# Right-side SBUF tiles moved down by 32 bytes in a hybrid encoder block on one core

## The chip, the core and the metric

The kernel runs on one core of one Trainium2 chip. The metric is the device time of one execution in microseconds, and the time of a kernel is the median of its runs. A profiled execution also gives a span, from the first to the last instruction on the core, which is a little shorter than the device time.

## What is computed

One layer of a bidirectional encoder is applied to two batches with shared weights: a prompt of 512 tokens and a sample of 256, which the kernel treats as 768 rows. The width is 2048 and everything is float32.

```
h = rmsnorm(x); z = h @ w_in                  # [fourier 1024 | q 1024 | k 256 | v 256]
of = fourier_mix(zf, w_f)                     # Re(2-D DFT over positions, channels), 8 groups
q, k = rope(q), rope(k)                       # 16 query heads, 4 key heads, width 64
oa = window_attention(q, k, v, sink)          # each token sees +-128 positions, plus a sink
x = x + concat(rmsnorm(of), rmsnorm(oa)) @ w_out
h = rmsnorm(x)
u = relu(h @ w_up); x = x + (u * u) @ w_down  # 2048 -> 8192 -> 2048
y = rmsnorm(x)
```

## The kernel before

Every large product is done as three matmuls on TensorE. Each operand is split into a high part (rounded to the format that the matmul reads, by ScalarE) and a low part (the rest, by VectorE), and high x high, high x low and low x high are added in PSUM. In the profile, tiles with an `h` at the end of the name hold high parts, those with an `l` low parts.

The work goes through these stages, in this order.

- **v** (line 222): the value projection, accumulated for all six blocks of 128 rows. The result is split into `vhl`.
- **z** (line 546): the input projection. A weight piece `wh` or `wl` is the stationary operand (the one that is loaded into the array, the profile's PEld rows), and a half of the rows, 384 columns of `hh` or `hl`, is the moving operand (the one that streams through). The Fourier group (lines 331, 363, 384) and the rotation of keys and queries are interleaved.
- **attention and first output projection**: scores (line 588, stationary `qs`, moving `kdl` or `kdh`), transposes of the probabilities (line 642), their product with the values (line 659, stationary `vhl`, moving `th` or `tl`), between steps of the output projection (line 743, 512 moving columns of `wh` or `wl`). A planner written in the kernel sets the order of this stage. The second half of the output projection follows, with transposes of its result (line 132), which fill `xf`.
- **up** (line 1038): `h @ w_up` with a seven-product scheme of the Strassen kind. Stationary are `wh` and `wl`, moving are 384 columns of `xf`, or of `xs` for one of the seven products in the second half.
- **down** (line 1325): `(u*u) @ w_down`, 512 moving columns of `wh` or `wl`, then the final norm and the stores.

SBUF holds 128 partitions, and a tile occupies the same bytes of each. Tile pools are stacked from two ends: most of them from the low addresses up (left), and those opened with `side="right"` from the high addresses down. These are the pools on the right:

```python
vp = vctx.enter_context(tc.tile_pool(name="vp", bufs=1, side="right", reuse_waits="tile"))
vhl = vp.tile([P, NM, NKV, 2, HD], F32R, tag="vhl", name="vhl")
...
kp = kt["kp"] = kctx.enter_context(tc.tile_pool(name="kp", bufs=1, side="right", reuse_waits="tile"))
...
tp = tctx.enter_context(tc.tile_pool(name="tp", bufs=1, side="right", reuse_waits="tile"))
xf = tp.tile([P, 7, 2, 4, HALF], F32R, tag="xf", name="xf")
...
bp = bctx.enter_context(tc.tile_pool(name="bp", bufs=1, side="right", reuse_waits="tile"))
```

`kp` holds the mask, the tables of the rotation (`cosr`, `sinr`), `sink`, the keys (`kdh`, `kdl`), the rotation's work tiles (`rx`, `ry`, `rh`, `rl`) and the queries (`qs`). `bp` holds `cx`, from which `xf` is split. A fifth pool on the right holds `xs`, which takes the first of the seven factors of the second half while `xf` is still in use. `vp` and `kp` are closed after the attention, and `tp` then starts at the same edge.

The right edge lies at byte 229344 of a partition, which is 32 more than a multiple of 64. Every tile on the right has a size that is a multiple of 64 bytes, so each of them starts at 32 more than a multiple of 64: `vhl` at 217056, `kdl` at 187360, `kdh` at 175072, `xf` at 143328, `xs` at 131040. On the left most tiles that matmuls read start at a multiple of 64 (`wh` from 9984, `wl` from 30464, `hh` from 59136, `hl` from 71424, `th`, `tabh`, `cwh`); those of the Fourier group behind an odd-sized tile (`sh` at 195360, `sl`, `ah`, `al`, `ofh`, `ofl`) start at 32 more.

The matmul of the up stage and the reads of its moving operand:

```python
xb = right[kh][s]          # xf[:, factor], in the second half also xs
for t in range(2):
    for i in range(4):
        for n, (w, o) in enumerate(((wh, 0), (wh, 1), (wl, 0))):
            nc.tensor.matmul(ps[:, t, :HALF], w[:, i, t * P : (t + 1) * P], xb[:, o, i, :], ...)
```

Of the kernel before, what the change touches and what calls it, by code (L numbers as in the profile page):

```python
# [11 lines left out]
F32 = mybir.dt.float32  # L12
# [8 lines left out]
P = 128  # L21
# [19 lines left out]
def hybrid_encoder(ctx: ExitStack, tc: tile.TileContext, a: dict):  # L41
# [7 lines left out]

    cpool = ctx.enter_context(tc.tile_pool(name="cpool", bufs=1))  # L50
    wpool = ctx.enter_context(tc.tile_pool(name="wpool", bufs=1))
    dpool = ctx.enter_context(tc.tile_pool(name="dpool", bufs=1, space=DRAM))

    ident = cpool.tile([P, P], F32, tag="ident", name="ident")
# [989 lines left out]
    right = [[xf[:, f] for _, f, _ in steps]]  # L1044
# [492 lines left out]
```

## Time and profile before

| | us |
|---|---|
| median of three runs | 2595.88 (2594.96 to 2597.75) |
| the profiled execution | 2596.02 |
| its span on the core | 2594.2 |
| TensorE busy in the span | 2578.1 |
| VectorE, ScalarE, GpSimd busy | 1706.9, 1057.5, 245.3 |

Busy times overlap across engines. A matmul's shown duration is longer than its share of the time, since matmuls are pipelined; how fast they follow each other is read from a stretch of the chain of work that ended last, as its time divided by the number of matmuls in it. The granted TensorE clock is 0.999 of full speed.

### The profile page before, as it was taken

Reading aid. Unit: us, or ns where it says so; the run is one execution under the profiler, and the core shown is the slowest. Engines: PE = TensorE matmul, PEld = TensorE weight load, DVE = VectorE, ACT = ScalarE, POOL = GpSimd, SP = SyncE. Lnnn points to the kernel's source line nnn. Section 1 sums busy time; section 2 is a strip of 40 time slices with the busy share of each in tenths; the row PEclk is TensorE's granted clock in tenths of the full one; section 3 lists DMA queues with packets and bytes.
Section 4 is the critical chain, followed back from the end, with each engine's and each line's share of the span. In section 5 each row is a group of like instructions: output and inputs, shape, how many; then the busy total and the mean of one; then the engine's idle time right before and its main releaser. Section 6 shows DMA issues by size and latency. Waiting matters only on the chain.

```text
span 2594.2 us, 34860 instructions
## 1 busy us (share of the span) xinstructions
PE 2578.1 (99%) x13556; PEld 2364.2 (91%) x13556; DVE 1706.9 (66%) x2088; ACT 1057.5 (41%) x1506; POOL 245.3 (9%) x356
## 2 busy tenths in 40 slices
PE   9999999999999999999999999999999999999998
PEld 9999998888899999999999999988888888888886
DVE  5344546775555656656777877667776765777678
ACT  6233316664333334333544454433333333333335
POOL 1011213332100101000000000010000000000000
PEclk9999999999999999999999999999999999999999
DMA  8333577558864445547666666685543662554364
GB/s 306 121 114 127 164 226 220 146 149 215 221 199 165 163 157 191 184 158 302 211 216 227 231 215 221 214 332 178 187 154 111 217 232 80 177 187 154 100 206 154
DMA packets 277621, 488.22 MB, mean 188 GB/s; under 512 B 21200, under 2 KB 169552, under 8 KB 276432
## 3 DMA queue, kind: packets, MB, share of 16 engines
q1 hardware_dynamic: 201904, 330.89, 39.7%
q10 hardware_dynamic: 53632, 95.86, 9.6%
q0 software_dynamic: 21920, 59.26, 8.3%
q8 instruction: 106, 1.74, 0.3%
q14 instruction: 59, 0.48, 0.1%
HBM read 359.30 MB, written 126.62 MB: 187 GB/s over the span
## 4 chain that ended last, share of the span: by engine, by line
PE 98%; DMA 0%; issue 0%; DVE 0%; ACT 0%; POOL 0%; POOLq 0%; ACTq 0%; DVEq 0%
PE pu L1038 36%; PE pd L1325 35%; PE pz L546 12%; PE pm L743 10%; PE pv L222 1%; PE s L588 1%; PE o L659 1%; PE t L642 1%; PE pa L363 1%; PE pe L384 0%; PE ptx L132 0%; DMA raw<-in_w_out 0%; PE pc L331 0%; PE pz L384 0%; DMA wr<-in_w_v 0%
## 5 line engine op out<-in xcount | busy, mean ns | idle before, releaser
L1038 PE MATMUL pu<-xf,wh 128*128 128x384 f32 x3328 | 847.5, 336 | 0.0
L1038 PEld LDWEIGHTS pu<-xf,wh 128*128 128x128 f32 x3328 | 601.2, 188 | 0.1
L1038 PE MATMUL pu<-xf,wl 128*128 128x384 f32 x1664 | 559.1, 336 | 0.0
L1325 PE MATMUL pd<-wh,sh 128*128 128x512 f32 x1320 | 513.5, 389 | 0.0
L1325 PE MATMUL pd<-wl,sh 128*128 128x512 f32 x1320 | 513.5, 389 | 0.0
L1325 PE MATMUL pd<-wh,sl 128*128 128x512 f32 x1320 | 513.5, 389 | 0.0
L1301 ACT ACTIVATE wh<-rd 128x1024 fp32r<-128x1024 f32 x200 | 211.9, 1060 | 514.2 <-PE pd L1325 277.2
L1311 DVE TENSOR_TENSOR wl<-rd,wh 128x1024 fp32r<-128x1024 f32 x200 | 242.8, 1223 | 216.3 <-ACT wh L1301 211.5
L1038 PEld LDWEIGHTS pu<-xf,wl 128*128 128x128 f32 x1664 | 312.8, 188 | 0.0
L1325 PEld LDWEIGHTS pd<-wh,sh 128*128 128x128 f32 x1320 | 247.7, 188 | 51.6
L1325 PEld LDWEIGHTS pd<-wh,sl 128*128 128x128 f32 x1320 | 247.7, 188 | 51.4
L1325 PEld LDWEIGHTS pd<-wl,sh 128*128 128x128 f32 x1320 | 247.8, 188 | 51.4
L1018 ACT ACTIVATE wh<-ur 128x1024 fp32r<-128x1024 f32 x160 | 169.6, 1060 | 253.9 <-DVE sm L1073 87.2
L1059 DVE TENSOR_TENSOR o<-pu,o 128x768 f32<-128x768 f32 x160 | 153.0, 956 | 165.2 <-PE pu L1038 152.4
L1024 DVE TENSOR_TENSOR wl<-ur,wh 128x1024 fp32r<-128x1024 f32 x160 | 195.3, 1220 | 49.6 <-ACT wh L1018 48.6
L546 PE MATMUL pz<-hh,wh 128*128 128x384 f32 x576 | 147.2, 336 | 0.0
L546 PE MATMUL pz<-hl,wh 128*128 128x384 f32 x576 | 146.3, 334 | 0.0
L546 PE MATMUL pz<-hh,wl 128*128 128x384 f32 x576 | 146.2, 334 | 0.0
L1294 DVE TENSOR_TENSOR rd<-rd 128x1024 f32<-128x1024 f32 x112 | 131.8, 1218 | 0.0
L1018 ACT ACTIVATE wh<-sx 128x1024 fp32r<-128x1024 f32 x64 | 67.9, 1062 | 117.6 <-DVE sx L1001 80.5
L1314 DVE TENSOR_TENSOR sl<-sr,sh 128x768 fp32r<-128x768 f32 x110 | 104.6, 951 | 0.0
L546 PEld LDWEIGHTS pz<-hl,wh 128*128 128x128 f32 x576 | 104.1, 188 | 0.0
(213 smaller groups left out, 3466.6 us busy)
## 6 DMA issues: line engine op xcount, KB each, us to landing
rd<-in_w_down SPq DMA_DIRECT2D x176, 512.0 KB, 4.2
ur<-in_w_up SPq DMA_DIRECT2D x128, 512.0 KB, 4.2
sr<-sd SPq DMA_DIRECT2D x94, 384.0 KB, 4.5
pd<-o ACTq DMA_DIRECT2D x64, 384.0 KB, 2.5
o<-pd POOLq DMA_DIRECT2D x64, 384.0 KB, 5.8
sd<-sm ACTq DMA_DIRECT2D x60, 384.0 KB, 2.5
raw<-in_w_in SPq DMA_DIRECT2D x36, 512.0 KB, 3.6
raw<-in_w_out SPq DMA_DIRECT2D x32, 512.0 KB, 5.0
```

The costliest lines, as they stand in the source:

```text
L222: nc.tensor.matmul(pv[m][:, :256], l[j][:, i, m * P : (m + 1) * P], wv[j][r][:, i, :], start=(k == 0 and n == 0), stop=(k == NK - 1 and n ...
L546: nc.tensor.matmul(ps[c][s][:, :HALF], w[:, i, cs], h[j][:, i, s * HALF : (s + 1) * HALF], start=first and n == 0, stop=last and n == 2,)
L743: nc.tensor.matmul(ps[:], l(k), w[:, k % 2, :], start=(k == 0 and n == 0), stop=(k == 7 and n == 2))
L1018: nc.scalar.activation(wh[:], raw[:], AF.Copy)
L1024: nc.vector.tensor_tensor(out=wl[:], in0=raw[:], in1=f32(wh[:]), op=ALU.subtract)
L1038: nc.tensor.matmul(ps[:, t, :HALF], w[:, i, t * P : (t + 1) * P], xb[:, o, i, :], start=(s == first_of[bank] and i == 0 and n == 0), stop= ...
L1059: nc.vector.tensor_tensor(out=o, in0=src, in1=o, op=ALU.add)
L1294: add = lambda x, y, op: nc.vector.tensor_tensor(out=x[:], in0=x[:], in1=y[:], op=op)
L1301: nc.scalar.activation(wh[:], t[:], AF.Copy)
L1311: nc.vector.tensor_tensor(out=wl[:], in0=t[:], in1=f32(wh[:]), op=ALU.subtract)
L1314: nc.vector.tensor_tensor(out=sl[:], in0=sr[:], in1=f32(sh[:]), op=ALU.subtract)
L1325: nc.tensor.matmul(out, l[:, q, ts], w[:, ns], start=(j == 0 and q == 0 and t == 0), stop=(j == HP // 2 - 1 and q == 1 and t == 2),)
```

## The change

One line is added after the pools `cpool` and `wpool`. It opens a pool on the right before all others and takes one tile of 8 floats (32 bytes in each partition) from it, which stays allocated to the end and is never written or read.

```diff
     cpool = ctx.enter_context(tc.tile_pool(name="cpool", bufs=1))
     wpool = ctx.enter_context(tc.tile_pool(name="wpool", bufs=1))
+    edge = ctx.enter_context(tc.tile_pool(name="edge", bufs=1, side="right")).tile([P, 8], F32, tag="edge", name="edge")
     dpool = ctx.enter_context(tc.tile_pool(name="dpool", bufs=1, space=DRAM))
```

In the built program every tile on the right starts 32 bytes lower: `vhl` at 217024, `kdl` at 187328, `kdh` at 175040, `xf` at 143296, `xs` at 131008, each now a multiple of 64 (and still not of 128). No tile on the left moves. The instructions, their order on each engine and their semaphore waits are those of before; the line numbers behind the new line are one higher.

## The prediction

> **What bounds the kernel now.** I first read the head of the page, for who is busy.
>
> ```profile
> span 2594.2 us, 34860 instructions
> PE 2578.1 (99%) x13556; PEld 2364.2 (91%) x13556; DVE 1706.9 (66%) x2088; ACT 1057.5 (41%) x1506; POOL 245.3 (9%) x356
> ```
>
> TensorE is idle for 2594.2 - 2578.1 = 16.1 us in all. Next I cut the span at the stage borders (the columns are the stretch, its length, and busy time of PE, PEld, DVE, ACT and POOL) to see where those 16 us lie.
>
> ```profile
> 0.00:43.00 43.00, 37.48 (x289) 37.49 (x290) 22.80 (x29) 30.29 (x39) 4.96 (x14) 1.00 0.92 346
> 43.00:282.00 239.00, 238.73 (x1479) 237.31 (x1478) 100.06 (x192) 73.53 (x154) 33.80 (x24) 1.00 0.40 129
> ...
> 386.00:738.00 352.00, 351.55 (x1779) 296.86 (x1779) 224.87 (x546) 186.36 (x453) 95.62 (x139) 1.00 0.72 192
> 738.00:1671.00 933.00, 933.00 (x5387) 932.84 (x5386) 634.64 (x612) 403.38 (x434) 70.49 (x129) 1.00 0.59 202
> 1671.00:2583.00 912.00, 912.00 (x4025) 755.18 (x4024) 662.96 (x618) 333.60 (x383) 20.56 (x34) 1.00 0.53 178
> 2583.00:2595.00 12.00, 1.32 (x6) 0.75 (x4) 4.96 (x10) 3.39 (x7) 0.55 (x1) 0.74 0.60 231
> ```
>
> Before 43 us it idles 43 - 37.48 = 5.5 us, after 2583 us 11.2 - 1.3 = 9.9 us up to the end of the span. In between there are only 0.27 + 0.45 = 0.7 us. The start works on `xk`, `wr` and `hh`, the end on `acc`; no tile of the right side is in either. So the change can gain in one way only, by a faster succession of matmuls, and can lose by that or by making TensorE wait. A busy PE is not yet a PE at its best pace, so the third view is the chain of work that ended last (start, length, what, how many), from which the pace is read.
>
> ```profile
> 98.91 8.32 PE pz L546 x48
> ...
> 281.17 104.11 PE pz L546 x600
> ...
> 434.29 8.43 DMA raw<-in_w_out
> ...
> 708.67 10.90 PE pm L743 x48
> ...
> 746.87 923.53 PE pu L1038 x5328
> 1670.40 905.77 PE pd L1325 x3996
> ```
>
> Up runs 5328 matmuls in one piece, 923.53 / 5328 = 173.33 ns each. Down runs 905.77 / 3996 = 226.67 ns each. From these two, 128 more columns cost 53.3 ns, or 0.417 ns a column, so 384 columns cost 160 ns and 13.3 ns come on top of each matmul; 512 columns give 213.3 and the same 13.3.
>
> **The change part by part.** The built program has the same instructions with the same waits, and other start addresses for the right-side tiles. The unused tile costs no instruction and no time. What can change is the duration of the accesses to moved tiles.
>
> *The moving reads of `xf` and `xs`.* These are 3328 + 1664 + 256 + 128 = 5376 matmuls, and by far the largest term: 1 ns on each is 5.4 us.
>
> ```profile
> L1038 PE MATMUL pu<-xf,wh 128*128 128x384 f32 x3328 | 847.5, 336 | 0.0
> L1038 PE MATMUL pu<-xf,wl 128*128 128x384 f32 x1664 | 559.1, 336 | 0.0
> L1325 PE MATMUL pd<-wh,sh 128*128 128x512 f32 x1320 | 513.5, 389 | 0.0
> L546 PE MATMUL pz<-hh,wh 128*128 128x384 f32 x576 | 147.2, 336 | 0.0
> ...
> L743 PE MATMUL pm<-wh,ofh 128*128 128x512 f32 x192 | 77.2, 402 | 0.0
> L743 PE MATMUL pm<-wh,oah 128*128 128x512 f32 x192 | 76.0, 396 | 0.0
> ...
> L1038 PE MATMUL pu<-xs,wh 128*128 128x384 f32 x256 | 65.2, 336 | 0.0
> L1038 PE MATMUL pu<-xs,wl 128*128 128x384 f32 x128 | 43.0, 336 | 0.0
> ...
> L659 PE MATMUL o<-th,vhl 128*128 128x512 f32 x56 | 22.6, 404 | 0.0
> L659 PE MATMUL o<-tl,vhl 128*128 128x512 f32 x56 | 22.2, 396 | 0.0
> ...
> L588 PE MATMUL s<-kdl,qs 128*128 128x256 f32 x64 | 16.6, 289 | 0.0
> L588 PE MATMUL s<-kdh,qs 128*128 128x256 f32 x64 | 16.2, 281 | 0.0
> ...
> L588 PE MATMUL s<-kdl,qs 128*128 128x384 f32 x32 | 11.3, 354 | 0.5 <-ACT p L623 0.5
> L588 PE MATMUL s<-kdh,qs 128*128 128x384 f32 x32 | 10.8, 336 | 0.0
> ```
>
> The kernel holds the answer already. The input projection (L546) has the same shape, 384 moving columns, the same kind of stationary tile, and its moving tiles `hh` (from byte 59136) and `hl` (from 71424) start at multiples of 64. So L546 is what L1038 will be after the change. Its pace in the chain is 104.11 / 600 = 173.52 ns, and 8.32 / 48 = 173.33 ns in the piece at 98.91. Against 173.33 the aligned reads are 0 to 0.19 ns slower, which on 5376 matmuls gives 0 to +1.0 us. The single durations agree, 336 ns on both lines. I take 0, from the piece that equals it to the hundredth.
>
> *The attention's operands `qs`, `kdl`, `kdh`, `vhl`.* The scores are 2 x 64 + 2 x 32 matmuls, the products with the values 112. Here matmuls of other lines stand between, so I bound by durations. If all that these groups have over the shortest row of their shape were due to the start address, the move would gain, for the scores, 64 x (289 - 281) + 32 x (354 - 336) = 1.1 us, and for the products 56 x (404 - 389) + 56 x (396 - 389) = 1.2 us, together 2.3 us. But `kdh` has the same start and shows no excess, and 402 and 396 ns also stand on line 743, where the moving tile `wh` starts at a multiple of 64 and no operand is on the right. On the side of a loss, taking the aligned line 743's spread, 402 - 389 = 13 ns, for all 304 matmuls gives +4.0 us. I take 0, since the likeness to line 743 and to 336 ns is nearest.
>
> *ScalarE and VectorE.* They write `xf`, `kdh`, `kdl` and `cx`, and read `mask`, `cosr`, `sinr`. The same shape on both sides:
>
> ```profile
> L67 ACT ACTIVATE xf<-cx 128x512 fp32r<-128x512 f32 x6 | 3.8, 632 | 12.7 <-DVE cx L919 12.7
> ...
> L67 ACT ACTIVATE tabh<-tab 128x512 fp32r<-128x512 f32 x2 | 1.3, 634 | 0.0
> ```
>
> ```profile
> L702 DVE TENSOR_TENSOR oal<-oar,oah 128x512 fp32r<-128x512 f32 x12 | 8.1, 689 | 9.4 <-ACT oah L700 9.4
> ...
> L68 DVE TENSOR_TENSOR xf<-cx,xf 128x512 fp32r<-128x512 f32 x6 | 4.1, 686 | 0.2
> ```
>
> ScalarE takes 632 ns into a tile at 32 over and 634 into one at a multiple of 64, VectorE 686 and 689. Even on a hundred instructions 3 ns are 0.3 us, and they lie beside matmuls: cost 0.
>
> *DMAs into and out of right-side tiles.* These rows give size and median time from issue to landing.
>
> ```profile
> raw<-in_w_out SPq DMA_DIRECT2D x32, 512.0 KB, 5.0
> ...
> xf<-x SPq DMA_DIRECT2D x6, 1536.0 KB, 11.6
> ...
> xk<-in_x_t SPq DMA_DIRECT2D x15, 384.0 KB, 7.2
> ...
> xt<-in_x_prompt SPq DMA_DIRECT2D x4, 1024.0 KB, 7.4
> ...
> qs<-ql SPq DMA_DIRECT2D x18, 128.0 KB, 3.6
> ...
> cosr<-in_c_cos SPq DMA_DIRECT2D x1, 384.0 KB, 5.7
> ```
>
> `xf` takes 11.6 / 1536 = 7.6 ns a KB at 32 over, `xt` 7.4 / 1024 = 7.2 at a multiple of 64. If the start made that difference, each load of `xf` would land 0.5 us earlier, and 3.0 us in all. No time follows, since matmuls wait for none of them:
>
> ```profile
> PE pv L222 <- ACT wh L67: 5.5, 1, 5.5
> PE s L588 <- ACT p L623: 0.5, 1, 0.5
> ```
>
> These are all the waits that the profile lists for TensorE, 6.0 us, and none is for a DMA. If that cover were gone, 0.5 us a load is what it could cost or gain.
>
> The Trainium skill has a rule that gives this term another size. "DMA: Bandwidth & Descriptors", section "How a descriptor splits into AXI transactions", says that a transfer that starts off a 256-byte boundary also pays for the bytes before its start, in steps of 32 bytes. The rows of `qs` are 512 bytes and go from 224 to 192 over such a boundary, and by that page I estimate 23 beats before and 22 after, 4% of at most 3.6 us, or 0.14 us. No run here shows it; by it the sum stays 0 too, and it speaks against the slower rival C below.
>
> *Sum.* 0 + 0 + 0 + 0 us, with bounds from -2.3 to +1.0 + 4.0 = +5.0. The profiled execution took 2596.02 us, its span 2594.2 and 1.8 around it; the median of the three runs, 2595.88, is 0.14 below it. I predict 2595.9.
>
> **The rivals.**
>
> *A, faster: the 13.3 ns are the price of a start off 64.* Then up would lose them, 5376 x 13.3 = 71.5 us, and the time would be 2524. For it: up is the largest stage and all its moving reads are off. Against it: down has the same 13.3 ns with `wh` and `wl` at multiples of 64, and L546 has 173.33 to 173.52. A start that mattered only from 128 or 256 bytes on would not be reached by the change, and that is no change in time.
>
> *B, faster by a little: the attention's excess goes.* The whole bound of 2.3 us gives 2593.6, which lies within 0.2% (5.2 us, about what a measurement of this kernel can tell from no change). So B cannot pass for faster; it is part of no change.
>
> *C, slower: the loads of `qs` land later and hold up the weights behind them.* The place is the piece of the chain at 434.29, where 8.43 us pass through a `raw` load of the output projection on SP's queue, against a median of 5.0. If transfers to the new addresses took longer, loads behind them would too. TensorE has work at hand there (351.55 of 352 us busy), and it would show only from some 5.2 us more, which is 62% longer than 8.43. At twice the time it gives 2595.9 + 8.4 = 2604.3. Against it: `cosr`, at 32 over, took 5.7 us, and `xk`, as large and at a multiple of 64, 7.2.
>
> *D: the change does nothing, since the tiles don't move.* In the built program all of them start 32 lower, so this is out.
>
> **How the numbers follow.** A gets 0.03, as the same shape has been seen at an aligned start. C and other waits of that kind get 0.04. No change, B within it, gets the rest, 0.93. Hence faster 0.03, same 0.93, slower 0.04. The range for 8 in 10 needs only the case of no change: the lower end is the bound of -2.3 with the 0.9 us by which the fastest of the three runs lay under the median, rounded down to 2592. The upper end is +5.0, 2601, which also holds the 1.9 us by which the slowest run lay over it.
>
> **What would show it right or wrong.** Right: in the chain of the changed kernel the piece of `pu` has again about 5328 matmuls in 923.5 us, and the durations of `pu`, `s` and `o` stay at 336, 336 to 354 and 396 to 404 ns. A pace of `pu` at 160 ns would show A, `kdl` at 336 and `vhl` at 389 ns would show B, and a new wait of TensorE for a DMA between 386 and 738 us would show C. Wrong in my reasoning would be any `pu` pace under 173.0 or over 173.9 ns, since then L546 is no stand-in for it, through its place in SBUF or its neighbours on other engines.

## The result: 17 us slower, in the up stage's matmuls

| | before | changed |
|---|---|---|
| median of five runs, us | 2596.16 (2594.96 to 2597.75) | 2613.61 (2612.05 to 2614.46) |
| span of the profiled execution, us | 2594.2 | 2612.5 |

The ratio is 1.0067, with a 95% interval of 1.0056 to 1.0078. The forecast was 2595.9, with 2592 to 2601. Among the runs further below one stands apart, 2737.87 us in the kernel both32, whose other nine took 2595.12 to 2601.48 us; its median and ratio leave that run out.

The chain of work that ended last of the changed kernel (start, length, what, how many matmuls), the pieces that answer to those shown of before:

```profile
281.00 104.11 PE pz L547 x600
...
709.04 10.90 PE pm L744 x48
...
747.39 941.28 PE pu L1039 x5328
1688.67 905.77 PE pd L1326 x3996
```

The input projection, the output projection and down take what they took, to the hundredth. Up goes from 923.53 to 941.28 us, that is from 173.33 to 941.28 / 5328 = 176.67 ns a matmul. On all 5376 matmuls 3.33 ns are 17.9 us, of the 18.3 by which the span grew. The groups of the changed kernel, with the mean duration of one matmul, say the same:

```profile
L1039 PE MATMUL pu<-xf,wh 128*128 128x384 f32 x3328 | 856.3, 338 | 0.0
...
L547 PE MATMUL pz<-hh,wh 128*128 128x384 f32 x576 | 147.4, 336 | 0.0
...
L1039 PE MATMUL pu<-xs,wh 128*128 128x384 f32 x256 | 65.9, 338 | 0.0
...
L660 PE MATMUL o<-th,vhl 128*128 128x512 f32 x56 | 22.6, 403 | 0.0
...
L589 PE MATMUL s<-kdl,qs 128*128 128x384 f32 x32 | 11.3, 354 | 0.4 <-ACT p L624 0.4
L589 PE MATMUL s<-kdh,qs 128*128 128x384 f32 x32 | 10.8, 336 | 0.0
```

And TensorE waits no longer than before, for no DMA. These are all the waits listed for it (total, times, longest):

```profile
PE pv L223 <- ACT wh L68: 5.0, 1, 5.0
PE pv L223 <- ACT hh L71: 0.5, 1, 0.5
PE s L589 <- ACT p L624: 0.4, 1, 0.4
```

They are 5.9 us in all, after 6.0 before, so no wait came in. Each matmul that streams `xf` or `xs` takes 3.33 ns more, although its moving operand now starts at a multiple of 64, like that of the input projection, which has 173.5 ns.

Nor do the other engines or the DMAs slow it. In up there are stretches in which neither VectorE, ScalarE and GpSimd nor any DMA is at work. One of them is shown from the kernel before and one from the changed kernel, each as the busy times of PE, PEld, DVE, ACT and POOL with the clock and the share and rate of the DMAs, and then as the chain in the same stretch:

```profile
1135.69:1137.93 2.24, 2.24 (x14) 2.24 (x14) 0.00 (x0) 0.00 (x0) 0.00 (x0) 1.00 0.00 0
...
1135.67 2.43 PE pu L1038 x14
```

```profile
1143.68:1145.96 2.28, 2.28 (x14) 2.28 (x14) 0.00 (x0) 0.00 (x0) 0.00 (x0) 1.00 0.00 0
...
1143.66 2.47 PE pu L1039 x14
```

The 14 matmuls take 2.43 / 14 = 173.6 ns each before and 2.47 / 14 = 176.4 after, so the loss is there with TensorE alone. Over all such moments of up in the changed kernel, 215 steps from the start of one matmul to the start of the next, the mean is 176.6 ns.

### The profile page after: what moved, and what is told of

Same layout as the page of the kernel before. It is cut to its first block, busy times and chain, and to the rows that moved or that the text cites. A ratio compares the mean times of both kernels' runs of the same rounds, so it can differ in the third digit from the quotient of the medians.

```text
span 2612.5 us, 34860 instructions
## 1 busy us (share of the span) xinstructions
PE 2596.4 (99%) x13556; PEld 2381.6 (91%) x13556; DVE 1706.1 (65%) x2088; ACT 1057.7 (40%) x1506; POOL 244.3 (9%) x356
## 4 chain that ended last, share of the span: by engine, by line
PE 99%; DMA 0%; issue 0%; ACT 0%; DVE 0%; SPq 0%; POOL 0%; POOLq 0%; DVEq 0%; ACTq 0%
PE pu L1039 36%; PE pd L1326 35%; PE pz L547 11%; PE pm L744 10%; PE pv L223 1%; PE s L589 1%; PE o L660 1%; PE t L643 1%; PE pa L364 1%; PE pe L385 0%; PE ptx L133 0%; DMA xk<-in_x_t 0%; PE pc L332 0%; PE pz L385 0%; DMA oadh<-ob 0%
## 5 line engine op out<-in xcount | busy, mean ns | idle before, releaser
L1039 PE MATMUL pu<-xf,wh 128*128 128x384 f32 x3328 | 856.3, 338 | 0.0
L1019 ACT ACTIVATE wh<-ur 128x1024 fp32r<-128x1024 f32 x160 | 169.4, 1059 | 257.3 <-DVE ur L1002 104.2
```

The costliest lines, as they stand in the source:

```text
L1019: nc.scalar.activation(wh[:], raw[:], AF.Copy)
```

## The experiments

In what follows a start is given as what it has over a multiple of 256 bytes. The distance is the start of the moving operand less that of the stationary one, also over a multiple of 256. Every step within the tiles of up is a multiple of 512 bytes (512 and 1024 in `wh`, 1536, 6144 and 12288 in `xf`), so a tile's start holds for all its matmuls. That 256 is the period was not tested: counted over 512 instead, all distances of up below stay the same numbers, but for one slot and `xs` in stagger_left32 (480 in place of 224).

In these terms, the input projection before has moving 0, stationary 0, distance 0. Up has moving 224, stationary 0, distance 224, and in the changed kernel 192, 0 and 192. Two theories fit these three: **M**, that the moving start counts, and **D**, that the distance counts.

**Only the left side moved (left32).** The large tiles of the left side go up by 32, and the right side stays.

```diff
     wpool = ctx.enter_context(tc.tile_pool(name="wpool", bufs=1))
+    left = wpool.tile([P, 8], F32, tag="left", name="left")
```

> The kernel before with the large tiles of the left side 32 bytes higher and the right side where it was: xf stays at 224 over a multiple of 256, wh and wl go to 32, so the distance is 192 as in the changed kernel, but xf itself has not moved. Theory M: up keeps 173.33 ns a matmul, and the time stays at 2596, unless hh at 32 costs something in the input projection. Theory D: up goes to 176.67 ns and the time to about 2614; the input projection, where hh moves with wh, keeps 173.5 ns.

Measured: median 2613.46 us, ratio 1.0069 (1.0054 to 1.0084). The chain of this kernel:

```profile
746.82 941.28 PE pu L1039 x5328
1688.10 905.77 PE pd L1326 x3996
```

`xf` has not moved, its start is no multiple of 64, and up takes the 941.28 us of the changed kernel. This is against M, and as D has it.

**Both sides moved (both32).** A tile of 32 bytes, `mhalf`, is taken from the left side and put at the right edge in place of the unused one, so that the large tiles of both sides go down by 32.

```diff
+    edge = ctx.enter_context(tc.tile_pool(name="edge", bufs=1, side="right"))
...
-    mhalf = cpool.tile([P, 8], F32, tag="mhalf", name="mhalf")
+    mhalf = edge.tile([P, 8], F32, tag="mhalf", name="mhalf")
```

> One tile of 32 bytes of the left side is put at the right edge, so that the right side moves down by 32 bytes as in the changed kernel and the large tiles of the left side too: xf at 192 over a multiple of 256, wh and wl at 224, the distance 224 as in the kernel before. Theory M: xf at 192 makes up run at 176.67 ns, about 2614. Theory D: up at 173.33 ns, the time that of before, about 2596.

Measured: median 2596.6 us, ratio 1.0005 (0.9995 to 1.0015). The chain:

```profile
283.73 104.11 PE pz L547 x600
...
749.25 923.70 PE pu L1039 x5328
1672.95 905.77 PE pd L1326 x3996
```

`xf` starts where it does in the changed kernel, and up has its 173.4 ns back. With left32 this decides for D and against M: moving either operand by 32 costs 17 us, moving both costs nothing.

**Seven distances in one kernel (stagger, stagger_left32).** Each of the seven factor slots of `xf` is made 32 bytes longer, and the matmuls of each slot get a line of their own. The second kernel also has the `left` tile of left32.

```diff
-    xf = tp.tile([P, 7, 2, 4, HALF], F32R, tag="xf", name="xf")
+    xf = tp.tile([P, 7, 8 * HALF + 8], F32R, tag="xf", name="xf")
+    xf = xf[:, :, : 8 * HALF].rearrange("p f (o i t) -> p f o i t", o=2, i=4)
...
```

> The kernel before, with each of the seven factor slots of xf made 32 bytes longer, so that the slots start at 0, 32, 64, 96, 128, 160 and 192 over a multiple of 256 (xs at 0), while the stationary tiles wh and wl stay at 0. The matmuls of each slot are written on a line of their own. Theory M (the start of the moving operand alone sets the pace, and starts at an odd multiple of 64 are slow): slots 2 and 6 (64 and 192) at 176.67 ns a matmul, the other five and xs at 173.33. Theory D (the distance from the start of the stationary operand to that of the moving one sets it): slot 6 at 176.67 and slot 0 at 173.33 by the two traces at hand, the others open, and not bound to multiples of 64. Theory O (the addresses don't matter, and something else moved with the tiles, such as another engine's access): slots need not differ, all at one pace.

> The staggered slots of xf again, with all large tiles of the left side, wh and wl among them, 32 bytes higher, so that the stationary tiles start at 32 over a multiple of 256. Theory M: every slot has the pace that it has in the staggered kernel without the shift, and xs too. Theory D: the paces move on by one slot, so that slot 1 has what slot 0 had, slot 2 what slot 1 had, and so on; slot 0 and xs (now 224 from the stationary start) have 173.33 as in the kernel before.

In the first run of the staggered kernel every matmul was some 3.6 times as long, also where nothing was changed (600 of the input projection took 369.79 us). It says nothing on the slots, and the kernel was run again.

> The seven factor slots of xf at 0, 32, 64, 96, 128, 160 and 192 over a multiple of 256 and xs at 0, the stationary tiles at 0, each slot's matmuls on a line of their own, as before. Theory D, from the paces of the shifted staggered kernel at the same distances: 0, 32, 64 and 160 at 173.2 to 174.5 ns a matmul, 96 at 176.7, 128 at 176.2, and 192 at 176.67 as in the changed kernel. In slots: 0, 1, 2 and 5 fast, 3, 4 and 6 slow. Theory M, that the moving start alone decides: slots 4 and 5 slow (they were in the shifted kernel), 3 fast.

The chain of the repeated run in a window of the first half; a piece is one product of 24 matmuls with one slot (lines 1046, 1048, ..., 1058 are slots 0 to 6):

```profile
847.28 4.16 PE pu L1050 x24
851.44 4.19 PE pu L1058 x24
855.63 4.16 PE pu L1046 x24
859.79 4.16 PE pu L1048 x24
863.95 4.17 PE pu L1056 x24
868.12 4.24 PE pu L1052 x24
872.36 4.22 PE pu L1054 x24
```

And of the kernel with the left side moved (lines 1047, 1049, ..., 1059 are slots 0 to 6):

```profile
843.51 4.24 PE pu L1055 x24
847.75 4.16 PE pu L1051 x24
851.91 4.16 PE pu L1059 x24
856.07 4.17 PE pu L1047 x24
860.24 4.18 PE pu L1049 x24
864.42 4.22 PE pu L1057 x24
868.65 4.16 PE pu L1053 x24
```

Sorted by distance, in us for 24 matmuls (4.16 is 173.3 ns each):

| distance | 0 | 32 | 64 | 96 | 128 | 160 | 192 | 224 |
|---|---|---|---|---|---|---|---|---|
| left side at 0 | 4.16 | 4.16 | 4.16 | 4.24 | 4.22 | 4.17 | 4.19 | |
| left side at 32 | 4.18 | 4.16 | 4.16 | 4.24 | 4.22 | 4.16 | | 4.17 |

The rows agree by distance. By slot they don't: slot 3 (moving start 96) takes 4.24 in one kernel and 4.16 in the other, slot 5 (160) takes 4.17 and 4.22. M is refuted, also in the form that odd multiples of 64 are slow. One number is off: the distance 192 gave 4.19, 174.6 ns, and not 176.67. It is no remnant of the product ahead of it, since by the starts of its matmuls in the trace the first 12 and the last 12 have the same mean, 174.5 and 174.6 ns. The distance 192 thus has more than one pace. The 4.17 and 4.18 do come from such a remnant: of the first seven matmuls after the change of distance some take up to 185 ns, and from the eighth on all have 173.3.

**Only the stationary tiles moved, with `raw` beside them (w32_up).** It is left32 with a gap of 224 bytes ahead of the up stage's own tiles, which brings them back.

```diff
     up = up_ctx.enter_context(tc.tile_pool(name="up", bufs=1, reuse_waits="tile"))
+    up.tile([P, 56], F32, tag="gap", name="gap")
```

> In the up stage only the weight tiles (wh, wl and the loaded raw beside them) start at 32 over a multiple of 256; xf stays at 224, and the tiles that the other engines read and write there (ur, sx, o, sm) are brought to a multiple of 256 again by a gap of 224 bytes. Theory D: it is the stationary operand, so up runs at 176.67 ns and the time is about 2614. Rival theory E: it is a collision of the reads of xf with another engine's accesses to the other left tiles, which are where they were before: up at 173.33 ns, time 2596.

The chain within up:

```profile
746.81 932.82 PE pu L1039 x5280
```

This is 932.82 / 5280 = 176.67 ns, so the tiles that were brought back have no part in it, and theory E falls. `raw` stayed moved, but only the other engines and the DMAs touch it, and here too a stretch of up without any of them (14 matmuls in 2.47 us) has the slow pace. The one time was 2618.41, 4 us over the expected 2614. Of these, 2.0 us are a new wait at the start of down, and some 0.5 us are the 72 matmuls there with `osh` and `osl`, whose distance became 32: their rows went from 389 to 395 ns. In up 32 is fast, so with 512 columns other distances may be slow, or the period is not 256 (counted over 512 it is 288 here). The rest was not followed.

```profile
PE pd L1327 <- ACT sh L1307: 2.0, 1, 2.0
```

```profile
L1327 PE MATMUL pd<-wh,osh 128*128 128x512 f32 x24 | 9.5, 395 | 0.0
```

**The same distance in other stages (hh192_sh64).** The input projection and down get the distance 192, up stays at 224.

```diff
         hp = ph.enter_context(tc.tile_pool(name="hp", bufs=1, reuse_waits="tile"))
+        hp.tile([P, 48], F32, tag="gap", name="gap")
...
     epool = ep["p"] = ctx.enter_context(tc.tile_pool(name="ep", bufs=1, reuse_waits="tile"))
+    epool.tile([P, 16], F32, tag="gap", name="gap")
```

> The up stage is left as it was before. In the input projection hh and hl start at 192 over a multiple of 256 and the stationary tiles at 0; in the down stage the stationary sh and sl start at 64 and the moving wh and wl at 0, but for the first two units. Both distances are then 192. Theory D, if it holds for every line: 3.33 ns on 1728 matmuls of the input projection, 176.8 ns a matmul and 5.8 us, and 3.33 ns on some 3900 of down, 230 ns a matmul and 13 us: 2596 + 19 = about 2615. If the effect belongs to the up stage's order of matmuls alone (two with the same stationary tile behind each other, one bank): both stages keep 173.5 and 226.67 ns, time 2596.

Measured: median 2625.4 us, ratio 1.0116 (1.01 to 1.0133). The chain:

```profile
65.69 33.92 PE pz L547 x192
100.05 8.49 PE pz L547 x48
...
143.65 8.33 PE pz L547 x48
...
283.54 104.91 PE pz L547 x600
...
749.42 923.62 PE pu L1039 x5328
1673.04 934.73 PE pd L1326 x4008
```

It isn't up's order of matmuls: both stages slow down and up does not. But the size is not one number. The input projection changes between two paces, 33.92 / 192 = 176.7 ns and 8.33 / 48 = 173.5, and has 174.9 over the long piece, near the 174.6 of the staggered kernel. What makes it switch was not found. Down, with 512 columns, takes 934.73 / 4008 = 233.2 ns against 226.67, so 6.5 ns more and twice what was expected.

**Other starts by the same line (edge64, edge96).** The unused tile of the change is made 64 and 96 bytes long.

```diff
-... side="right")).tile([P, 8], F32, tag="edge", name="edge")
+... side="right")).tile([P, 16], F32, tag="edge", name="edge")    # edge96: [P, 24]
```

> The changed kernel with an unused tile of 64 bytes in place of 32: xf and the right side start at 160 over a multiple of 256, again no multiple of 64. Theory D, from the staggered kernels at the distance 160 (173.3 and 173.9 ns a matmul): up at most 3 us longer than before, time 2596 to 2599.

> The changed kernel with an unused tile of 96 bytes: the right side starts at 128 over a multiple of 256, so xf is at a multiple of 128. Theory D, from the staggered kernels at the distance 128 (175.8 and 176.2 ns): 13 to 16 us more in up, time 2609 to 2612. If a rounder start were what helps, it would be no slower than before, 2596.

Measured: edge64 2596.6 us, ratio 1.001 (0.9997 to 1.0024); edge96 2609.46 us, ratio 1.0051 (1.0036 to 1.0066). The chain of edge64, then that of edge96:

```profile
747.42 923.54 PE pu L1039 x5328
```

```profile
745.78 937.72 PE pu L1039 x5328
```

At 32 over a multiple of 64 up is as fast as before, at a multiple of 128 it takes 176.0 ns a matmul. A rounder address is not what helps. One of the ten runs of edge64 took 2613.52 us, the others 2596.2 to 2599.45; there is no trace of it, and it is not explained.

**Which stationary tile counts (wl32).** Only `wl` and what lies above it go up by 32, so that of three matmuls the third has the distance 192, and its load runs beside the second.

```diff
+                    wv[j] = [wpool.tile([P, 4, 256], F32R, tag="wh", name="wh", bufs=5)]
+                    if j == 0:
+                        wpool.tile([P, 8], F32, tag="gap", name="gap")
+                    wv[j].append(wpool.tile([P, 4, 256], F32R, tag="wl", name="wl", bufs=5))
...
```

> The kernel before with wl, and all that lies above it on the left, 32 bytes higher, and wh where it was; in up the three matmuls of a turn (high x high, high x low, low x high) are on lines of their own. xf stays at 224, so the distance is 224 for the two with wh and 192 for the one with wl. Theory D-own: a matmul's distance to its own stationary tile counts, and the third (low x high) is the slow one, 3.3 ns or more above 173.33. Theory D-next: the distance to the stationary tile of the matmul behind it counts, whose load runs beside it, and the second (high x low) is the slow one. Other stages change their distances too, so the total tells nothing here.

The groups by line (1047 is the first of the three matmuls, 1049 the second, 1051 the third) have these mean durations of one:

```profile
L1049 PE MATMUL pu<-xf,wh 128*128 128x384 f32 x1664 | 564.1, 339 | 0.0
L1047 PE MATMUL pu<-xf,wh 128*128 128x384 f32 x1664 | 561.6, 338 | 0.0
L1051 PE MATMUL pu<-xf,wl 128*128 128x384 f32 x1664 | 560.8, 337 | 0.0
```

The second is the longest, by 1 and 2 ns over the others. The starts of the matmuls in the trace say more: from the first to the second it is 175.0 ns on average, from the second to the third 177.5, and from the third to the next first 174.2. Of the 6.7 ns that the three have over 3 x 173.33, 4.2 lie where the second streams and `wl` is loaded, 1.7 beside the first and 0.8 beside the third. D-own is refuted, since the third has the least. D-next has the largest part right, and not all of it.

The one time was 2643.43 us, and the other stages of this kernel set a limit to D:

```profile
284.15 105.44 PE pz L549 x600
...
668.40 11.19 PE pm L746 x48
...
1691.01 935.21 PE pd L1334 x4008
```

The input projection takes 175.7 ns a matmul here, the output projection 233.1 and down 233.3, where before it was 173.5, 227.1 and 226.7. For 512 columns, as in the last two, the distance 224 of `wh` was not seen elsewhere. But the input projection has 384 columns, and its distances are 32 with `wh` and 0 with `wl`, at which up is fast. New in this kernel is that `wh` and `wl` differ in their starts, so that the distance changes from one matmul to the next. A matmul's own distance alone does not set the pace, then; the table holds for stretches in which all matmuls have the same one.

## Why the prediction was wrong

- **What bounds the kernel** held: TensorE does, no new wait came, and 17.9 of the 18.3 us lost are in the pace of matmuls. The prediction had said that this is the one way in which the change could gain, and one of two in which it could lose.
- **The step that failed** is in the largest term: "So L546 is what L1038 will be after the change." It was taken as a stand-in because its moving operand starts at a multiple of 64. But its stationary operand starts there too, and what counts in up is the distance between the two, which left32, both32 and w32_up show. In L546 this distance is 0. In L1038 it was 224, just as fast, and became 192. No matmul with 384 columns and that distance was in the kernel before, so the bounds 0 to +1.0 us came from a row that did not match; the term was +17.9. That L546 equalled L1038 to the hundredth was a coincidence of two different distances that are both fast.
- **The attention's operands**: taken at 0 in a range of -2.3 to +4.0. Their rows stand at 403, 354 and 336 ns after 404, 354 and 336. Both operands of the scores moved together; of the products only `vhl` moved, which took their distance from 32 to 64. This term and those of ScalarE, VectorE and the DMAs are borne out by the stages that kept their times.
- **The rivals.** A (13.3 ns less) is out: over all eight distances no product of up got below 4.16 us for 24. B (the attention's excess) did not go, and C (a wait) did not come. None of them was the slower case that happened. The remark at the end of the prediction, that a pace over 173.9 ns would mean that L546 is no stand-in "through its place in SBUF", names the place of the error and was not given a chance of its own.
- **The chances**: 0.04 for slower rested on waits alone. The profile of before showed loads of the second operand beside the matmuls for 932.84 of 933 us in up, and 3.33 ns on 5376 matmuls is enough, so a rival with that operand belonged in the list.
- **The DMAs**: TensorE had no DMA wait before or after, as said, so no run shows what the start of a transfer costs. The rule of the Trainium skill ("DMA: Bandwidth & Descriptors", section "How a descriptor splits into AXI transactions") on transfers off a 256-byte boundary stays untested here.

What is not settled is how the loss comes about. That the load of a stationary tile and the stream of a moving one hinder each other in SBUF would fit the distance and the place of the largest loss in wl32; it is inferred and not shown. Nor is there a rule that gives the pace from the starts: 192 has more than one pace, and in wl32 the distances 0 and 32, each fast by itself, are slow in turn.

## What to carry to other kernels

When tiles are moved, compare the starts of both operands of the matmuls that bound the time, not one tile's alignment, and keep tiles that take turns as an operand (`wh`, `wl`) at the same start; a row may stand in for another only if it agrees in all that the change touches. Where matmuls follow each other without a gap, read the pace from a long piece of the chain, before and after any edit of the allocation, since 2 ns in a duration were 17 us here. In these runs no distance made up faster than it was, so the kernel before stays the best: keep its tiles where they are, and look at the pace again whenever a tile is added ahead of `wh` or `xf`.

## What was not expected of the hardware

- The pace of 384-column matmuls in up depends on the distance between the starts of the stationary and the moving operand: 173.3 ns at 0, 32, 64, 160 and 224 over a multiple of 256 (up to 174.5 over 24 matmuls just after another distance), 175.8 to 176.7 at 96 and 128, and 174.6 or 176.7 at 192. The slow pace is there with TensorE alone at work, too (176.4 ns over 14 matmuls).
- With 512 columns the distance 192 costs 6.5 ns a matmul (226.67 to 233.2), with 384 columns 3.3, and in the input projection one distance gave both 173.5 and 176.7 ns within one execution.
- With `wh` and `wl` 32 bytes apart, matmuls of 384 columns whose distances are 32 and 0 in turn took 175.7 ns in place of 173.5, though either distance is fast by itself.
